# Routed rows finished one expert earlier, indirect transfers in written order, and four residual stores on another queue

## The chip, the cores and the metric

One core of one Trainium2 chip. The metric is the device time of one execution in microseconds; the number before is the median of three runs. The trace is one profiled execution of the same program.

## The reference, cut to what matters

One layer of an encoder trunk on 512 tokens (and 16 meta tokens) of width 1024. After the mixer and its layer norm comes a mixture of experts and a second layer norm, and the change is in that last part alone:

```python
grp_score = lax.top_k(grp, TOP_K)[0].sum(-1)      # 4 groups of 4 experts
sel = jnp.argmax(grp_score, axis=-1)              # one group for a token
topv, topi = lax.top_k(jnp.where(in_grp, scores, -1.0), TOP_K)   # two experts of it
for e in range(N_EXPERTS):                        # 16
    h = jax.nn.silu(t @ w_gate[e]) * (t @ w_up[e])
    out = out + comb[:, e:e + 1] * (h @ w_down[e])
h = layer_norm(DN_ALPHA * h + ffn, ln2_g[i], ln2_b[i])
```

Both experts of a token are of one group, so experts of different groups have no token in common.

## The kernel before, in words

The mixture works expert by expert, at most 96 tokens of each in the main path. `order` (L935) takes one expert of each group in turn (0, 4, 8, 12, 1, 5, ...), so four neighbours in it belong to four groups; below, "expert 12" means place 12 of `order`, and 15 is the last. For each place the kernel gathers the token rows from `h1_dram` into `XG` (L1505, an indirect DMA from GpSimd), transposes them (`xprep`, L1113) into `xT` (`x_out`, L1076: four parts on ScalarE, four on VectorE), multiplies by the gate and up weights (`gu`, L1101, and `gu_third` for tokens 65 to 96, in a branch on the count), applies silu (`act`, L1148), transposes the result (`htr`, L1274, copied to `hT` by ScalarE), multiplies by the down weights (`down`, L1299) and adds the weighted result to `o_dram` by two indirect DMAs that accumulate (`add_rows`, L1350). The weights stream from DRAM on SyncE's queue (`fetch`, L1239) into slots of 1 MB that are reused in turn.

`o_dram` first receives the residual rows: four tiles of 128 tokens, scaled on VectorE and stored from GpSimd (L1205 to L1208). `XG[0]` is then set to zero (L1253) and the rows of place 2 are gathered into it.

At the end the second layer norm is made by the class `Finish` (L1409). `out` already holds the bias of the norm, and each result is added to it by a scattering DMA. The four token tiles are loaded back from `o_dram` (L1530) after the scatters of place 12, normalised as a whole, and stored with the index `rest` (L1039), which sends the tokens of the last three experts out of bounds; the rows of places 13, 14 and 15 are gathered from `o_dram` (`rows_of`, L1555), normalised and stored by their own indices. From L1539 on VectorE and ScalarE execute in the order in which the code is written. In that order `xprep` of place 15 comes before the statistics of the tiles (L1565 to L1567), and the tiles' scaling on ScalarE (L1575) comes after `htr` of place 14. A scatter into `o_dram` waits until the tile loads have read it. The last expert is computed in split precision (`down_split`, L1323), whose two halves of output feed the last norm.

## Time and profile before

| | |
|---|---|
| median of three runs | 1038.21 us (1037.29 to 1038.98) |
| the profiled execution | 1038.58 us |
| its span in the trace | 1036.8 us |
| TensorE busy | 946.0 us, 91% of the span |
| mean granted TensorE clock | 0.969 |
| DMA over the whole span | 199.43 MB, 192 GB/s |

Times in the rows are microseconds from the span's start; busy and mean times of single instructions include their fixed part. The text in brackets at the end of a timeline row is the idle time of that engine before it and what ended it. L89 is the line of a helper that records instructions in written order, so those rows are told apart by their tiles: `gu` and `py` are the results of the gate or up and of the down products, `pt` transposes, `ys` the weighted rows, `raw` and `hb` the slots.

### The profile page before, as it was taken

What the parts mean: (1) busy time and instruction counts of PE and PEld (TensorE: products, weight loads), DVE (VectorE), ACT (ScalarE), POOL (GpSimd) and SP (SyncE); (2) the same over time, 40 slices, a digit from 0 to 9 for tenths busy, and PEclk for the clock granted to TensorE, in tenths of its full rate; (3) what the DMA queues carried; (4) which work ended last, traced back from release to release, by engine and by line L of the source; (5) the groups of instructions that cost most, each with busy time, mean ns of one, the idle gap of its engine ahead of it and who ended that gap; (6) DMA issues with size and microseconds to landing.
All of it is one profiled execution on the core that took longest, in us unless ns stands there. A gap on an engine that the chain in (4) does not pass through costs nothing. (4 is left out here: it accounts for less than half of the span.)

```text
span 1036.8 us, 19979 instructions
## 1 busy us (share of the span) xinstructions
PE 946.0 (91%) x8460; PEld 757.0 (73%) x8460; DVE 594.0 (57%) x1180; ACT 350.5 (34%) x503; POOL 167.5 (16%) x150
## 2 busy tenths in 40 slices
PE   4879999999999999999999897999779788999980
PEld 3878888999899898989898785877545344564550
DVE  6877671376869696978878778666520101001173
ACT  4344332532435252433425353224112121112252
POOL 4930000000000000000000226200212121212343
PEclk9999999999999999999999998999989899999996
DMA  7442446422323142333332423977899999999744
GB/s 220 138 162 100 131 131 178 122 82 82 134 90 128 56 151 74 123 102 123 102 122 72 153 91 133 379 290 304 293 367 372 373 373 374 371 372 373 251 123 78
DMA packets 98739, 199.43 MB, mean 192 GB/s; under 512 B 10272, under 2 KB 56968, under 8 KB 97616
## 3 DMA queue, kind: packets, MB, share of 16 engines
q1 hardware_dynamic: 83392, 163.78, 44.8%
q0 software_dynamic: 9392, 18.61, 7.2%
q10 hardware_dynamic: 5856, 15.61, 4.1%
q8 instruction: 76, 1.25, 0.5%
q14 instruction: 23, 0.19, 0.1%
HBM read 185.79 MB, written 19.79 MB: 198 GB/s over the span
## 5 line engine op out<-in xcount | busy, mean ns | idle before, releaser
L255 DVE TENSOR_TENSOR wl<-raw,wh 128x2048 fp32r<-128x2048 f32 (+1 forms) x49 | 111.7, 2283 | 53.2 <-ACT wh L252 53.0
L252 ACT CAST wh<-raw 128x2048 fp32r<-128x2048 f32 (+1 forms) x49 | 87.9, 1798 | 143.6 <-PE ss L800 64.1
L307 PE MATMUL mm<-hH,wh 128*128 128x264 f32 x624 | 128.7, 287 | 6.1 <-ACT ze L599 5.4
L89 PE MATMUL gu<-raw,xT 128*32 128x256 f32 (+1 forms) x2592 | 126.8, 344 | 7.8 <-issue 4.0
L307 PE MATMUL mm<-hH,wl 128*128 128x264 f32 x624 | 128.0, 286 | 0.0
L307 PE MATMUL mm<-hL,wh 128*128 128x264 f32 x624 | 127.3, 285 | 0.0
L89 PEld LDWEIGHTS gu<-raw,xT 128*32 128x32 f32 x2592 | 82.8, 110 | 48.8 <-issue 16.8
L1153 DVE TENSOR_TENSOR sg<-sg,gu 128x128 f32<-128x128 f32 x13 | 3.7, 288 | 182.5 <-ACT sg L1152 182.5
L307 PEld LDWEIGHTS mm<-hH,wh 128*128 128x128 f32 x624 | 99.1, 190 | 9.4 <-ACT ze L599 5.6
L809 POOL TENSOR_TENSOR acc<-acc,pre 128x512 f32<-128x512 f32 x12 | 19.1, 1614 | 530.5 <-ACT pre L808 530.5
L325 PE MATMUL mm<-hH,wh 128*128 128x512 f32 x256 | 102.5, 401 | 0.0
L325 PE MATMUL mm<-hL,wh 128*128 128x512 f32 x256 | 101.6, 397 | 0.0
L325 PE MATMUL mm<-hH,wl 128*128 128x512 f32 x256 | 101.5, 396 | 0.0
L307 PEld LDWEIGHTS mm<-hH,wl 128*128 128x128 f32 x624 | 98.0, 189 | 1.2 <-DVE wl L255 0.2
L307 PEld LDWEIGHTS mm<-hL,wh 128*128 128x128 f32 x624 | 97.4, 189 | 0.2
L89 PE MATMUL py<-raw,hT 128*32 128x512 f32 (+1 forms) x704 | 73.8, 558 | 5.2 <-issue 4.6
L800 PE MATMUL ss<-wh,yy 128*128 128x512 f32 x192 | 67.3, 410 | 0.0
L89 PEld LDWEIGHTS py<-raw,hT 128*32 128x32 f32 x704 | 23.5, 116 | 46.2 <-issue 39.2
L325 PEld LDWEIGHTS mm<-hH,wl 128*128 128x128 f32 x256 | 48.2, 188 | 10.5
L325 PEld LDWEIGHTS mm<-hH,wh 128*128 128x128 f32 x256 | 48.1, 188 | 10.3
L325 PEld LDWEIGHTS mm<-hL,wh 128*128 128x128 f32 x256 | 48.0, 188 | 10.3
L1256 POOL DMA_INDIRECT o_dram<-ys,ixq x26 | 40.5, 1557 | 74.3 <-ACT ys L1354 70.7
(391 smaller groups left out, 1584.1 us busy)
## 6 DMA issues: line engine op xcount, KB each, us to landing
raw<-in_w_exp_down_dram SPq DMA_DIRECT2D x30, 1024.0 KB
raw<-in_w_in_dram SPq DMA_DIRECT2D x28, 1024.0 KB
raw<-in_w_exp_up_dram SPq DMA_DIRECT2D x28, 1024.0 KB
raw<-in_w_exp_gate_dram SPq DMA_DIRECT2D x26, 1024.0 KB
M<-aD ACTq DMA_DIRECT2D x8, 1024.0 KB
raw<-in_w_in_dram SPq DMA_DIRECT2D x16, 512.0 KB
raw<-in_w_ssd_out_dram SPq DMA_DIRECT2D x8, 1024.0 KB
ze<-eD ACTq DMA_DIRECT2D x16, 256.0 KB
```

The source lines that it names most:

```text
L89: return lambda *a, **k: self.tc.keep_in_program_order(f(*a, **k))
L252: A.copy(wh[:, c], src[:, c])
L255: (E[i] if E else V).tensor_sub(wl[:, c], src[:, c], wh[:, c])
L307: T.matmul(ps[:, i, :HF], lhsT=w[:, k, cs], rhs=h[k][:, i * HF:(i + 1) * HF], start=(n == 0), stop=(n == 3 * KT - 1))
L325: T.matmul(ps, lhsT=w[:, k, cs], rhs=h[k][:, NM:], start=(n == 0), stop=(n == 3 * KT - 1))
L800: T.matmul(ps, lhsT=y[:, j, t * 128:(t + 1) * 128], rhs=w[:, j, hf * 512:(hf + 1) * 512], start=(n == 0), stop=(n == 5))
L809: G.tensor_add(a, a, f)
L1153: V.tensor_mul(sg[:, 256:384], sg[:, 256:384], p3[:, 128:])
L1256: return G.indirect_dma_start(out=dst, out_offset=off(ix), in_=src[:n], in_offset=None, **lim(dst), **kw)
```

## The change

Three things. The residual's four stores are issued by ScalarE instead of GpSimd. The tiles are loaded one expert earlier, after the scatters of place 11, and `rest` leaves out the tokens of the last four experts; the rows of place 12 are gathered and finished by themselves. And from the last gather of `h1_dram` on, the indirect DMAs of GpSimd are issued in the order of the code. With that the written order of VectorE and ScalarE changes: the statistics and scales of the tiles come first, ahead of `act` of place 14 and `xprep` of place 15, and the scaling of the four tiles comes ahead of `add_rows` of place 13.

```diff
@@ -258,12 +258,23 @@
         return bass.IndirectOffsetOnAxis(ap=ix, axis=0)
 
 
+
+    queue = []
+
+    def queued(f):
+        if not queue:
+            return f()
+        with tc.issue_after(queue[-1]):
+            r = f()
+        queue.append(r.ins)
+        return r
+
     def lim(v):
         return dict(bounds_check=v.shape[0] - 1, oob_is_err=False)
 
     def gather(dst, src, ix):
         n = ix.shape[0]
-        return G.indirect_dma_start(out=dst[:n], out_offset=None, in_=src, in_offset=off(ix), **lim(src))
+        return queued(lambda: G.indirect_dma_start(out=dst[:n], out_offset=None, in_=src, in_offset=off(ix), **lim(src)))
 
 
     with ExitStack() as p1:
@@ -1036,7 +1047,7 @@
 
             with tc.high_priority(offset=-3000):
                 rf, r1 = tokf[:, t:t + 1], small("rf")
-                for e_ in order[-3:]:
+                for e_ in order[-4:]:
                     o_ = rest[:, t:t + 1] if e_ == order[-1] else r1
                     V.scalar_tensor_tensor(o_, ohs[:, t, e_:e_ + 1], float(FAR), rf, op0=OP.mult, op1=OP.add)
                     rf = o_
@@ -1205,7 +1216,7 @@
             for t in range(NT):
                 V_.tensor_mul(vt[t], vt[t], g1B)
                 V_.tensor_add(vt[t], vt[t], b1B)
-                G.dma_start(o_dram[t * 128:(t + 1) * 128, :], vt[t])
+                A.dma_start(o_dram[t * 128:(t + 1) * 128, :], vt[t])
 
 
     rawz = ctx.enter_context(tc.tile_pool(name="rawz", bufs=RZ, reuse_waits="tile"))
@@ -1253,7 +1264,7 @@
     G.memset(XG[0], 0.0)
     def scatter(dst, src, ix, **kw):
         n = ix.shape[0]
-        return G.indirect_dma_start(out=dst, out_offset=off(ix), in_=src[:n], in_offset=None, **lim(dst), **kw)
+        return queued(lambda: G.indirect_dma_start(out=dst, out_offset=off(ix), in_=src[:n], in_offset=None, **lim(dst), **kw))
 
 
     gu3 = psG.tile([128, 256], F32, name="gu3", bufs=1)
@@ -1411,7 +1422,7 @@
 
 
         def __init__(self, rows, junk):
-            self.rows, self.junk, self.n = rows, junk, len(rows)
+            self.rows, self.junk, self.n = rows, junk, len(rows) + 1
 
             self.mv = mo.tile([128, self.n, 2], F32, name="mvf", bufs=1)
             self.rs = mo.tile([128, 4, self.n], F32, name="rsf", bufs=1)
@@ -1513,10 +1524,12 @@
         if i == 1:
             with tc.issue_after(last_[V]):
                 overflow()
+        if i == last - 2:
+            break
         add_rows(down(i - 1, fetch(wd[order[i - 1]], 256)), i - 1)
 
 
-    i, e = last - 1, order[last - 1]
+    w2, e = fetch(wd[order[last - 3]], 256), order[last - 1]
     wg2, wu2, w3 = fetch(wg[e], 512), fetch(wu[e], 512), fetch(wd[order[last - 2]], 256)
     wg_, wp_ = fetch(wg[order[last]], 512), fetch(wd[e], 256)
     wu_, wd_ = fetch(wu[order[last]], 512), fetch(wd[order[last]], 256)
@@ -1525,18 +1538,41 @@
     Q.dma_start(gb2[0], bcast_row(ln2_g, D))
     fv = [slot((128, 2, D)) for _ in range(4)]
     fv = [v[:, k, :] for v in fv for k in range(2)]
-
     for t in range(NT):
         last_['SP'] = Q.dma_start(fv[t], o_dram[t * 128:(t + 1) * 128, :]).ins
-    rows3 = fv[NT:NT + 3]
-    for v in rows3:
+    rows4 = fv[NT:]
+    for v in rows4:
         G.memset(v, 0.0)
-    gather(XG[(i + 1) % 2], h1_dram[:, :], ix_of(i + 1))
+    queue.append(gather(XG[last % 2], h1_dram[:, :], ix_of(last)).ins)
+
+
+    i = last - 1
+    V, A, G = (InOrder(tc, e_) for e_ in (V, A, G))
+
+    def rows_of(k, n):
+
+        ins = gather(rows4[k], o_dram[:, :], ix_of(last - 3 + k)).ins
+        if n:
+            apart(ins, n)
+        gets.append(ins)
+
+    def add_to(p, k):
+        for sc in add_rows(p, k):
+            for g_ in gets:
+                tc.declare_no_dep(sc, g_, reason="experts of different groups have no token in common")
+
+    gets = []
+    fin = Finish(fv[:NT] + rows4[:3], None)
+    add_to(down(i - 2, w2), i - 2)
+    rows_of(3, 1)
+    rows_of(0, 0)
+    for t in range(NT):
+        fin.stats(t)
+    fin.scales(slice(0, NT))
     pg = gu(wg2)
     count(i)
     htr(hs.pop(i - 1))
     pu = gu(wu2)
-    V, A, G = (InOrder(tc, e_) for e_ in (V, A, G))
     hs[i] = act(pg, pu, p3=gu_third(i, (wg2, wu2)))
     xprep(XG[(i + 1) % 2])
     us = [[slot((128, 2, D), F32R) for _ in range(2)] for _ in range(2)]
@@ -1546,71 +1582,63 @@
     spare = [spare[:, 2 * k:2 * k + 2] for k in range(2)]
     after = nu[0]
     on = spare[1]
+    fin.rows.append(fl(on))
+    fin.junk = fl(spare[0])
+    for t in range(NT):
+        fin.scaled(t)
+        fin.gain(t)
+    fin.store(0, rest[:, 0:1])
+    add_to(down(i - 1, w3), i - 1)
+    for t in range(1, NT):
+        fin.store(t, rest[:, t:t + 1])
     V.memset(fl(on)[CAP:], 0.0)
-    for w, (wh, wl) in zip(wd_, us):
-        A.copy(wh, w)
-        V.tensor_sub(wl, w, wh)
-    add_rows(down(i - 1, w3), i - 1)
-
-    def rows_of(k, ins, n):
-
-        ins.append(gather(rows3[k], o_dram[:, :], ix_of(last - 2 + k)).ins)
-        return ins[-1]
-
-    gets = []
-    apart(rows_of(2, gets, 2), 2)
-    rows_of(0, gets, 0)
-    fin = Finish(fv[:NT] + rows3[:2] + [fl(on)], fl(spare[0]))
-    tiles = slice(0, NT)
-    for t in range(NT):
-        fin.stats(t)
-    fin.scales(tiles)
+
+    def part(k):
+        A.copy(us[k][0], wd_[k])
+        V.tensor_sub(us[k][1], wd_[k], us[k][0])
+
+    part(0)
+    fin.stats(NT)
+    fin.scales(slice(NT, NT + 1))
     pg = gu(wg_)
     count(last)
     htr(hs.pop(i))
     sg = silu(pg)
-    for sc in add_rows(down(i, wp_), i):
-        for g_ in gets:
-            tc.declare_no_dep(sc, g_, reason="experts of different groups have no token in common")
-    for t in range(NT - 1):
-        fin.scaled(t)
-        fin.gain(t)
-    for t in range(2):
-        fin.store(t, rest[:, t:t + 1])
-    rows_of(1, gets, 0)
+    part(1)
+    add_to(down(i, wp_), i)
+    rows_of(1, 1)
+    fin.scaled(NT)
+    fin.gain(NT)
+    fin.store(NT, ix_of(last - 3))
+    rows_of(2, 0)
     act(None, gu(wu_), p3=gu_third(last, (wg_, wu_)), sg=sg)
     htr_split(sg, hhl)
     A.activation(epsq, epsc, AF.Sqrt)
     py = down_split(us, hhl)
-    fin.scaled(NT - 1)
-    fin.gain(NT - 1)
-    for t in range(2, NT):
-        fin.store(t, rest[:, t:t + 1])
-    fin.sums(NT)
-    fin.stats(NT + 1)
-    two, end = slice(NT, NT + 2), slice(NT + 2, NT + 3)
-    w_, og, st = col_of(wsl, last)[:CAP], rows3[2], bn_tile()
+    fin.sums(NT + 1)
+    fin.scales(slice(NT + 1, NT + 2))
+    fin.scaled(NT + 1)
+    fin.stats(NT + 2)
+    w_, og, st = col_of(wsl, last)[:CAP], rows4[3], bn_tile()
+    for hf in range(2):
+        V.scalar_tensor_tensor(on[:CAP, hf, :], py[hf], w_, og[:CAP, hf * 512:hf * 512 + 512], op0=OP.mult, op1=OP.add)
+        V.bn_stats(st[:, hf, :], on[:, hf, :])
+        if not hf:
+            fin.gain(NT + 1)
+            fin.store(NT + 1, ix_of(last - 2))
+    V.bn_aggr(fin.mv[:, NT + 3, :], st)
+    two = slice(NT + 2, NT + 4)
     fin.root(two)
-    V.scalar_tensor_tensor(on[:CAP, 0, :], py[0], w_, og[:CAP, 0:512], op0=OP.mult, op1=OP.add)
-    V.bn_stats(st[:, 0, :], on[:, 0, :])
     fin.steps(two)
-    V.scalar_tensor_tensor(on[:CAP, 1, :], py[1], w_, og[:CAP, 512:], op0=OP.mult, op1=OP.add)
-    V.bn_stats(st[:, 1, :], on[:, 1, :])
-    fin.scaled(NT)
-    V.bn_aggr(fin.mv[:, NT + 2, :], st)
-    fin.root(end)
-    fin.gain(NT)
-    fin.store(NT, ix_of(last - 2))
-    fin.steps(end)
-    fin.scaled(NT + 1)
-    fin.gain(NT + 1)
-    fin.store(NT + 1, ix_of(last - 1))
-
-    A.activation(og, fl(on), AF.Identity, bias=fin.rs[:, 3, NT + 2:NT + 3], scale=fin.rs[:, 0, NT + 2:NT + 3])
-    fin.rows[NT + 2] = og
-    fin.gain(NT + 2)
-    fin.store(NT + 2, ix_of(last))
+
+    A.activation(og, fl(on), AF.Identity, bias=fin.rs[:, 3, NT + 3:NT + 4], scale=fin.rs[:, 0, NT + 3:NT + 4])
+    fin.rows[NT + 3] = og
+    fin.scaled(NT + 2)
+    for n in (3, 2):
+        fin.gain(NT + n)
+        fin.store(NT + n, ix_of(last - 3 + n))
     V, A, G, Q, T = plain
+    queue.clear()
     with tc.issue_after(last_['SP']):
         last_['SP'] = Q.dma_start(gb2[1], bcast_row(ln2_b, D)).ins
 
```

## Rows read from the trace of the kernel before

**Rows 1.** The page: its span.

```profile
span 1036.8 us, 19979 instructions
```

**Rows 2.** Timeline of TensorE (PE), places 1 to 3: start, us, what, idle before.

```profile
739.52 0.55 PE L89 MATMUL pt<-ident,sg 128*128 128x128 f32 x3
...
746.11 1.58 PE L89 MATMUL gu<-raw,xT 128*32 128x128 f32 x49 [0.28 <-issue]
...
756.94 1.53 PE L89 MATMUL pt<-ident,xg 96*128 96x96 f32 x8 [9.25 <-DMA xg<-h_dram,idx]
...
764.51 1.90 PE L89 MATMUL gu<-raw,xT 128*32 128x256 f32 x32
...
775.63 1.20 PE L89 MATMUL pt<-ident,xg 96*128 96x96 f32 x8
...
781.95 3.64 PE L89 MATMUL gu<-raw,xT 128*32 128x256 f32 x64
```

**Rows 3.** Timeline of GpSimd (POOL) in the same stretch.

```profile
746.69 0.97 POOL L1253 MEMSET xg<- 128x1024 f32 x1
...
747.94 1.01 POOL L266 DMA_INDIRECT xg<-h_dram,idx  x1 [0.28 <-POOL xg L1253]
```

**Rows 4.** Stretches: length, busy of PE, PEld, DVE, ACT, POOL, clock, DMA share, GB/s.

```profile
735.00:966.00 231.00, 203.27 (x3279) 117.66 (x3283) 36.57 (x116) 43.62 (x113) 55.84 (x45) 0.94 1.03 373
...
966.00:979.00 13.00, 11.14 (x163) 6.08 (x155) 1.85 (x6) 3.49 (x9) 5.45 (x5) 1.00 0.61 227
...
808.50:815.00 6.50, 6.46 (x32) 2.45 (x36) 1.85 (x6) 1.67 (x5) 1.01 (x1) 0.51 1.03 408
```

**Rows 5.** Timeline of SyncE's queue (SP), the last loads.

```profile
960.70 1.98 SPq L1525 DMA_DIRECT2D raw<-in_ln_g_dram  x1
...
981.28 2.41 SPq L1530 DMA_DIRECT2D raw<-o_dram  x4
```

**Rows 6.** Timeline of GpSimd (POOL), scatters of places 11 and 13.

```profile
958.58 1.55 POOL L1256 DMA_INDIRECT o_dram<-ys,ixq  x1 [0.30 <-issue]
...
991.50 1.56 POOL L89 DMA_INDIRECT o_dram<-ys,ixq  x1 [12.29 <-DMA raw<-o_dram]
```

**Rows 7.** Timeline of VectorE (DVE), place 14 and the tiles.

```profile
983.04 1.24 DVE L89 TENSOR_SCALAR xT<-pt,gb 128x96 f32<-128x96 f32 x4 [0.63 <-PE pt L89]
...
994.47 1.23 DVE L89 BATCH_NORM_STATS2 st<-raw 128x6 f32<-128x512 f32 x2
...
995.73 0.21 DVE L89 BATCH_NORM_AGGREGATE mvf<-st 128x2 f32<-128x12 f32 x1
```

**Rows 8.** Timeline of ScalarE (ACT), places 13 and 14.

```profile
983.89 3.71 ACT L89 CAST raw<-raw 128x2048 fp32r<-128x2048 f32 x2
...
992.32 0.48 ACT L89 COPY hT<-pt 128x384 f32<-128x384 f32 x1 [3.48 <-PE pt L89]
...
996.56 1.05 ACT L89 ACTIVATE ys<-py,wq 128x512 f32<-128x512 f32 x2 [3.48 <-PE py L89]
...
998.36 3.51 ACT L89 ACTIVATE raw<-raw,rsf 128x1024 f32<-128x1024 f32 x3 [0.75 <-DVE rsf L89]
```

**Rows 9.** Timeline of TensorE (PE): down products, and the split one.

```profile
810.00 6.06 PE L89 MATMUL py<-raw,hT 128*32 128x512 f32 x32
...
992.85 3.64 PE L89 MATMUL py<-raw,hT 128*32 128x512 f32 x32 [0.62 <-ACT hT L89]
...
1007.32 5.80 PE L89 MATMUL pye<-raw 128*96 128x512 f32 x24 [1.60 <-ACT raw L89]
```

**Rows 10.** The last chain: ACT, DVE, DVE, then POOL.

```profile
1009.83 1.04 ACT L89 ACTIVATE raw<-hb 128x1024 f32<-128x1024 f32 x1
...
1012.53 0.73 DVE L89 SCALAR_TENSOR_TENSOR raw<-pye,wsl,raw 96x512 f32<-96x512 f32 x1
...
1019.91 1.23 DVE L89 TENSOR_TENSOR raw<-raw 128x1024 f32<-128x1024 f32 x1 [0.22 <-ACTq L1623]
...
1022.75 1.43 POOL L89 DMA_INDIRECT out_dram<-raw,idx  x1 [0.30 <-issue]
```

## The prediction

> **What bounds the kernel now.** I read the page first [rows 1]: the span is 1036.8 us, the profiled time 1038.58 us, so 1.78 us lie outside it; the profile is 0.37 us above the median of 1038.21 us. TensorE is busy for 91% of the span, so the next view was its timeline. Through the experts it runs almost without a gap, with one exception: after the products of place 1 end at 747.69 it stands for 9.25 us until the rows `xg` of place 2 have come [rows 2]. GpSimd's timeline shows why: the memset of `XG[0]` starts at 746.69, right behind the last residual store, and the gather only at 747.94 [rows 3].
>
> The stretches show a second resource at its limit. From 735 to 966 us the DMA engines are busy 1.03 of the time at 373 GB/s [rows 4]. Weights are fetched into slots well ahead, so in this profile TensorE does not wait for them; but the stream has an end of its own. Its last load, the gain of the norm, is issued at 960.70 [rows 5], and the transfers thin out between 966 and 979 us, 13 us at 227 GB/s, 2.95 MB [rows 4]. I read 979 as the time when the stream has landed.
>
> At the end TensorE leads: the copy of `hT` of place 14 ends at 992.80 [rows 8], its down product starts at 992.85, and the split product runs from 1007.32 to 1013.12 [rows 9]. After that a chain of VectorE and ScalarE ends at 1021.14 and GpSimd's last store is issued by 1024.18; the span ends 12.62 us later [rows 10, 1].
>
> **The change, part by part.**
>
> *Stores on ScalarE's queue.* ScalarE idles where they go, so issuing them costs nothing: its next work, the `hT` copy of place 0, has to wait for the same VectorE results. If that cover were missing, four issues would stand there, which cost SyncE 2.41 us for four loads [rows 5]. GpSimd loses four issues, and with them the waits ahead of the memset. The memset then needs only the transposes of `htr` of place 0, over at 740.07 [rows 2]: memset 740.1 to 741.1, gather 0.28 us later at 741.35 [rows 3]. From its start to TensorE's start took 9.00 us before (747.94 to 756.94). With the same 9.00 us the rows land at 750.35, 6.6 us earlier; at best they land before 747.7 and all 9.25 us go. Then the clock: from `xprep` to the next `gu` took 7.57 us after the gap and 6.32 us one place later [rows 2], so 1.25 us more. The gain at place 2 is 7.8 to 10.5 us; I take 9, for the data no longer stand behind 2 MB of stores in their own queue.
>
> The trace has these stores and the weights in flight together, at a busy share of 1.03 [rows 4]. The Trainium skill (DMA: Bandwidth & Descriptors, "Issuing engines are not separate DMA queues") says that DMAs of all issuing engines share the same 16 DMA engines, so that another issuer saves only sequencer time. By that rule the 9.00 us stay and only the earlier issue counts. That is the lower end above.
>
> *The tiles one expert earlier.* Scatter 11 is issued by 960.13 [rows 6], or some 9 us sooner, so its landing no longer decides. The four loads follow the gain of the norm on SyncE's queue, behind the stream that ends at 979. Price: 4 x 524,288 bytes at 408 GB/s, which a stretch of mere loads reached [rows 4], are 5.14 us: **the last tile lands at 984.1**. Lower end: if they fill the thin 13 us completely, (2.95 + 2.10 MB) at 373 GB/s after 966 give 979.5. Upper end: before, the scatter that waits for these loads started 10.22 us after their issue [rows 5, 6], which behind 979 gives 989.2. I take 984.1, as the loads queue behind a running stream and not into idle engines.
>
> Now VectorE's order counts. Statistics and scales stand ahead of `act` of place 14 and of `x_out` of place 15, which before ran at 983.04 [rows 7]. A tile's statistics take 1.47 us from first start to last end; the last tile is through at about 986.0. From there to ScalarE's first scaling went 2.42 us (995.94 to 998.36) [rows 7, 8]: 988.4. `x_out` comes after the scales, so TensorE, which with its 9 us would want it at about 979, stands until about 989.
>
> ScalarE's order is the longer chain. Four scalings at 1.17 us (three took 3.51): 993.1. `ys` of place 13, 1.05 us: 994.1. Half of the two casts, 1.86 us: 996.0. The `hT` copy of place 14, 0.48 us: 996.5 instead of 992.80 [rows 8]. **The down product of place 14 starts 3.7 us later than before, and the 9 us are gone.** What VectorE does meanwhile (gains, memset, one subtraction) is shorter than this chain and than TensorE's next products.
>
> *Clock.* TensorE now has idle stretches of some 8 and 3 us there. After the branch gap ahead of 808.5, the clock was 0.51, the 1.2 GHz level, from 808.5 to 815, and a down product of 32 matmuls took 6.06 us instead of 3.64 [rows 4, 9]. Between 0 and that I take the row: +2.4 us.
>
> *The tail.* B is the start of the split product (1007.32 before). The gathers of places 13 and 14 and GpSimd's longer row of stores end ahead of their users, as the tiles' stores are issued during the products. Before, the sums began at B + 2.5, after one scaling that is now gone, so now at about B + 1.5; two passes of 1.04 us [rows 10] with their small steps make some 2.6 us. Then VectorE in written order: scales of place 13 (bounded by the 2.42 us above; 2.2), statistics of place 14 (1.47): the first half of the last rows starts at B + 7.7, not B + 5.21 [rows 10]. From there to the end of the gain were 8.61 us; one block of six small steps (0.9) goes, a gain (1.2) moves off the root's shadow into the row; I take 8.2. Then a store starts at B + 16.2, a second one behind it ends at B + 19.5 instead of B + 16.86. With 12.0 us to the span's end (12.62 before, with more stores in flight) that is B + 31.5 instead of B + 29.5: +2.0 us, between 0 (if the sums and scales hide) and 3.
>
> `rest` with one more step per tile, a fourth memset, and a fourth gathered set of rows cost 0: they lie beside products. If the memset were late, only a gather would wait.
>
> **Sum:** 1038.58 + 3.7 + 2.4 + 2.0 = 1046.7 us on the profile's scale, 1046.3 on the median's. Its own range is 1039.5 (tiles at 979.5, clock kept) to 1051.4 (tiles at 989.2).
>
> **The rivals.**
>
> *The tiles are not late.* If the loads overtake the last weights, or the stream follows TensorE and ends 9 us sooner while VectorE fits its 8 us in ahead of place 14, the 9 us survive. For it: the slots come free earlier. Against: a share of 1.03 leaves the stream no room, and the loads stand last in the queue. It decides at about 976: from there down the kernel is faster, and below 969 nothing of the stall is left: 1038.2 - 9 + 2 = 1031, with part of the chain left up to 1036. Chance 0.20.
>
> *They land at the lower end, and the clock holds:* 1038.2 + 3.7 - 4.6 + 2.0 = 1039.3, no change that can be told. For it: the thin 13 us have room for all four tiles. Against: the transfers end on single engines, and a tile needs all. Chance 0.12.
>
> *The moved stores don't free the gather* (the memset or the rows wait for something else). Then TensorE comes to place 15 as before, at 983, waits for VectorE only some 6 us and keeps its clock: 1046.3 - 2.4 = 1043.9. Chance 0.10.
>
> **How the numbers follow.** The forecast has 0.58. A measurement of this kernel can tell some 0.2%, 2.1 us, from no change. Faster: the first rival, 0.20. Same: the second and the low edge of the forecast, 0.14. Slower: the rest, 0.66. The range must reach into the first rival, as 0.20 plus the top would be too much to leave out: 1034 to 1051.
>
> **What would show it.** Right: TensorE's 9.25 us gap gone or small; SyncE's tile loads issued about 963; the last tile's statistics at about 984; a gap of TensorE ahead of the second half of `gu` of place 15 until about 989, with the clock at 0.5; `hT` of place 14 copied at about 996; the split product from about 1013; the last store of GpSimd near 1033. Wrong: statistics of the tiles ending before 977, or a copy of `hT` of place 14 before 990; then the gain of place 2 reaches the end.

## The result, and the profile after

The changed kernel takes **1047.51 us** (median of four runs, 1046.83 to 1049.04) where the kernel before takes 1038.6 us beside it (1037.29 to 1040.06): ratio 1.0088, 95% interval 1.0073 to 1.0103. It is slower, as forecast, 1.2 us above the predicted 1046.3 and inside the range. The profiled execution took 1046.83 us, of which 1044.7 us are span, 7.9 us more than before [rows 1]. The page of the changed kernel:

```profile
span 1044.7 us, 20003 instructions
```

The two profiled executions do not start even. TensorE begins place 1 (the first `gu` of the expert loop) at 733.92 us after and at 735.92 us before; the change reaches nothing ahead of that. One row of the kernel before that the earlier groups do not hold, TensorE's timeline:

```profile
735.92 3.66 PE L89 MATMUL gu<-raw,xT 128*32 128x256 f32 x64 [1.07 <-ACT xT L1082]
```

So times within the experts are told below also as S+t, where S is that start (735.92 before, 733.92 after). TensorE's timeline of the changed kernel, from place 1 to the split product:

```profile
733.92 3.66 PE L89 MATMUL gu<-raw,xT 128*32 128x256 f32 x64 [1.07 <-ACT xT L1093]
...
748.09 1.49 PE L89 MATMUL pt<-ident,xg 96*128 96x96 f32 x8 [2.13 <-DMA xg<-h_dram,idx]
...
755.76 1.90 PE L89 MATMUL gu<-raw,xT 128*32 128x256 f32 x32
...
968.98 3.66 PE L89 MATMUL gu<-raw,xT 128*32 128x256 f32 x64 [0.34 <-DMA raw<-o_dram]
...
987.30 3.55 PE L89 MATMUL gu<-raw,xT 128*32 128x256 f32 x32 [2.21 <-DVE xT L89]
...
994.24 5.21 PE L89 MATMUL py<-raw,hT 128*32 128x512 f32 x32 [2.91 <-ACT hT L89]
...
1009.43 5.79 PE L89 MATMUL pye<-raw 128*96 128x512 f32 x24 [1.60 <-ACT raw L89]
```

At place 2 the gap is 2.13 us instead of 9.25 [rows 2], and the transposes of `xg` stand at S+14.17 instead of S+21.02. At the end stand two new waits that before did not have: 2.21 us for VectorE's `xT` inside `gu` of place 15, and 2.91 us for ScalarE's `hT` ahead of the down product of place 14. The split product starts at 1009.43, which is S+275.51 instead of S+271.40.

GpSimd's and ScalarE's timelines at place 1, then the last of VectorE's four residual tiles and the load of gate weights that SyncE issued last ahead of them:

```profile
738.13 0.95 POOL L1264 MEMSET xg<- 128x1024 f32 x1 [4.00 <-PE pt L89]
...
739.35 1.71 POOL L277 DMA_INDIRECT xg<-h_dram,idx  x1 [0.27 <-POOL xg L1264]
...
736.73 11.81 ACTq L1219 DMA_DIRECT2D o_dram<-v  x4
...
748.64 0.48 ACT L1291 COPY hT<-pt 128x384 f32<-128x384 f32 x1 [14.76 <-DMA raw<-in_w_exp_gate_dram]
...
742.65 1.22 DVE L89 TENSOR_TENSOR v<-v,b1B 128x1024 f32<-128x1024 f32 x1
...
731.79 0.37 SPq L228 DMA_DIRECT2D raw<-in_w_exp_gate_dram  x1
```

GpSimd sets `XG[0]` to zero as soon as TensorE's transposes are through and issues the gather at 739.35, 8.6 us sooner than before [rows 3], 6.6 by S. ScalarE stands among the four store issues for 11.81 us, and its copy of `hT` comes at 748.64. The row of 11.81 us is mostly waiting: in the trace each issue takes 0.33 us, the first three (736.73, 739.12, 741.51) start within 0.05 us of VectorE's tiles, and the fourth starts at 748.21 although its tile is ready at 743.87. What ended that last wait was the landing, at 748.14, of the gate weights that SyncE had issued at 731.79: by the trace the fourth store waits for the semaphore that this load counts up.

The tile loads on SyncE, and then the chain of VectorE and ScalarE that follows from them:

```profile
961.82 6.65 SPq L1542 DMA_DIRECT2D raw<-o_dram  x4
```

```profile
978.23 1.28 DVE L89 BATCH_NORM_STATS2 st<-raw 128x6 f32<-128x512 f32 x2 [13.54 <-SPq L1651]
...
983.73 0.21 DVE L89 BATCH_NORM_AGGREGATE mvf<-st 128x2 f32<-128x12 f32 x1
...
986.34 0.62 DVE L89 TENSOR_TENSOR sg<-sg,gu 128x256 f32<-128x256 f32 x2
...
986.87 1.23 DVE L89 TENSOR_SCALAR xT<-pt,gb 128x96 f32<-128x96 f32 x4
...
986.45 4.64 ACT L89 ACTIVATE raw<-raw,rsf 128x1024 f32<-128x1024 f32 x4 [7.38 <-DVE rsf L89]
...
993.71 0.47 ACT L89 COPY hT<-pt 128x384 f32<-128x384 f32 x1
```

The statistics start at 978.23, when the first tile has landed. (SyncE's L1651, which the profile names there, waits for the same landing; by these waits the last weights landed at 975.70, the gain of the norm at 976.96 and the first tile at 978.23, in the order of SyncE's queue.) They run without a gap for 5.7 us, and `act` of place 14 and the rows of place 15 come only behind the scales, at 986.34 and 986.87. ScalarE's scalings, `ys` of place 13 and half a cast follow one another to the copy of `hT` at 993.71. Of the stretches below, the first is the thin end of the stream with the tiles in it, the second what follows it, the last two the wait and the down product of place 14 (length, busy time of PE, PEld, DVE, ACT and POOL, granted clock, DMA share, GB/s):

```profile
966.00:979.00 13.00, 12.48 (x175) 6.59 (x171) 0.77 (x2) 3.42 (x9) 0.00 (x0) 0.97 0.82 326
...
979.00:985.00 6.00, 6.00 (x92) 2.61 (x81) 5.69 (x16) 0.08 (x1) 1.95 (x2) 1.00 0.18 44
...
985.00:994.20 9.20, 4.11 (x39) 1.69 (x35) 8.66 (x20) 7.75 (x9) 7.71 (x4) 0.81 0.26 52
...
994.20:999.60 5.40, 5.21 (x32) 1.15 (x32) 4.72 (x10) 2.13 (x3) 4.62 (x3) 0.70 0.79 130
```

With the tiles in it the thin end of the stream runs at 326 GB/s instead of 227 [rows 4], and behind 979 little is left. In the down product of place 14 the clock is 0.70, between its two levels.

The tail, GpSimd first, then ScalarE and VectorE:

```profile
982.74 1.55 POOL L89 DMA_INDIRECT o_dram<-ys,ixq  x1 [20.61 <-DMA raw<-o_dram]
...
1010.15 1.00 POOL L89 DMA_INDIRECT hb<-o_dram,idx  x1 [0.30 <-issue]
...
1013.94 1.01 POOL L89 DMA_INDIRECT raw<-o_dram,idx  x1 [1.02 <-DMA o_dram<-ys,ixq]
...
1014.30 1.06 ACT L89 ACTIVATE raw<-hb 128x1024 f32<-128x1024 f32 x1 [3.41 <-DMA hb<-o_dram,idx]
...
1016.99 0.15 DVE L89 TENSOR_SCALAR rsf<-mvf 128x1 f32<-128x1 f32 x1 [7.29 <-ACT raw L89]
...
1020.57 0.74 DVE L89 SCALAR_TENSOR_TENSOR raw<-pye,wsl,raw 96x512 f32<-96x512 f32 x1
```

GpSimd stands until 982.74, as its scatters of place 12 wait for the tile loads, and is then busy almost without a pause until the gather of place 14's rows at 1013.94. The rows of place 13 are gathered at 1010.15, and ScalarE's sums wait 3.41 us for them. The first half of the last rows starts at 1020.57, 11.1 us after the split product, where before it was 5.2 us [rows 9, 10]. From the start of the split product to the span's end go 35.3 us instead of 29.5.

The 7.9 us are thus, from front to back: 2.0 us gained ahead of place 1, 4.1 us lost from there to the split product, 5.8 us lost behind it.

### The profile page after: what moved, and what is told of

The parts are those of the page before. It is cut to its first block, busy times and chain, and to the rows that moved or that the text cites. A ratio compares the mean times of both kernels' runs of the same rounds, so it can differ in the third digit from the quotient of the medians.

```text
span 1044.7 us, 20003 instructions
## 1 busy us (share of the span) xinstructions
PE 952.4 (91%) x8460; PEld 757.5 (73%) x8460; DVE 598.3 (57%) x1200; ACT 351.0 (34%) x503; POOL 174.4 (17%) x149
## 3 DMA queue, kind: packets, MB, share of 16 engines
q8 instruction: 76, 1.25, 0.5%
## 5 line engine op out<-in xcount | busy, mean ns | idle before, releaser
L89 PE MATMUL py<-raw,hT 128*32 128x512 f32 (+1 forms) x704 | 78.4, 586 | 8.3 <-issue 5.2
L1267 POOL DMA_INDIRECT o_dram<-ys,ixq x24 | 37.3, 1553 | 71.0 <-ACT ys L1365 67.3
```

Of the source, the lines that this page charges most:

```text
L89: return lambda *a, **k: self.tc.keep_in_program_order(f(*a, **k))
L1267: return queued(lambda: G.indirect_dma_start(out=dst, out_offset=off(ix), in_=src[:n], in_offset=None, **lim(dst), **kw))
```

## The experiments

All times of a stage in this table come from the one profiled execution of each kernel, the ratio from its timed runs against the kernel before on the same chip. "hT" is the start of ScalarE's copy of place 14, "split" the start of the split product, "tail" from there to the span's end.

| kernel | S | hT | split | tail | median us | ratio, 95% interval |
|---|---|---|---|---|---|---|
| before | 735.92 | S+256.4 | S+271.4 | 29.5 | 1038.6 | |
| changed | 733.92 | S+259.8 | S+275.5 | 35.3 | 1047.5 | 1.0073 to 1.0103 |
| changed, again | 734.89 | S+258.6 | S+275.9 | 34.9 | 1049.3 | 1.0061 to 1.0129 |
| moved stores alone | 734.20 | S+249.3 | S+264.2 | 30.9 | 1034.2 | 0.9938 to 0.9981 |
| moved stores alone, again | 740.02 | S+252.2 | S+266.4 | 31.7 | 1035.6 | 0.9931 to 0.9976 |
| stores back | 737.20 | S+262.2 | S+278.9 | 35.1 | 1051.5 | 1.0079 to 1.0130 |
| rows of 13 first | 736.00 | S+259.5 | S+277.7 | 32.9 | 1048.6 | 1.0057 to 1.0105 |
| tiles behind | 733.74 | S+251.2 | S+277.4 | 38.6 | 1051.5 | 1.0082 to 1.0136 |
| VectorE back | 734.74 | S+260.7 | S+280.2 | 32.0 | 1049.1 | 1.0050 to 1.0115 |
| tiles by GpSimd | 736.93 | S+254.7 | S+269.3 | 36.8 | 1044.8 | 1.0027 to 1.0066 |
| rows of 13 second | 733.91 | S+258.9 | S+276.8 | 35.0 | 1050.0 | 1.0066 to 1.0135 |
| stores last | 735.24 | S+260.1 | S+275.8 | 32.1 | 1046.4 | 1.0042 to 1.0083 |
| all orders changed | 736.68 | S+249.0 | S+263.1 | 39.9 | 1040.1 | 0.9978 to 1.0035 |

### The two halves of the change apart

The kernel before with the moved stores and nothing else:

```diff
-                G.dma_start(o_dram[t * 128:(t + 1) * 128, :], vt[t])
+                A.dma_start(o_dram[t * 128:(t + 1) * 128, :], vt[t])
```

> Theory (the moved stores give TensorE time at place 2, and the new order at the end takes it away): the gap ahead of the transposes of place 2 falls from 9.25 us to about 2, TensorE is 5 to 7 us ahead from there, and since before's order at the end is led by TensorE, the lead reaches the end: 1031 to 1034 us. Rival (the weight stream has an end of its own, and a TensorE that is ahead only waits for weights): the lead melts until place 14, and the time stays at 1037 to 1039 us.

It takes 1034.17 us, 0.996 of the kernel before. TensorE's timeline, and the stretch in which the stream thins out:

```profile
748.06 1.17 PE L89 MATMUL pt<-ident,xg 96*128 96x96 f32 x8 [1.53 <-DMA xg<-h_dram,idx]
...
984.03 3.64 PE L89 MATMUL py<-raw,hT 128*32 128x512 f32 x32 [0.62 <-ACT hT L89]
...
998.42 7.10 PE L89 MATMUL pye<-raw 128*96 128x512 f32 x24 [1.60 <-ACT raw L89]
```

```profile
966.00:979.00 13.00, 12.82 (x187) 6.99 (x183) 4.75 (x8) 6.17 (x10) 3.79 (x3) 1.00 0.68 230
```

The gap at place 2 is 1.53 us, and in this profile the lead is there to the end: the down product of place 14 starts at S+249.8 instead of S+256.9, the split product 7.2 us sooner. The rival's melting lead does not happen here, though the stream thins out in the same stretch as before (230 GB/s; 227 before [rows 4]): the stream does have its own end, but in the old order no wait of TensorE at the end names it. Once more, on another chip:

> The moved stores alone once more, beside the kernel with all orders changed: 1032 to 1036 us, 3 to 6 us below the kernel before. By the rival (the first result owed itself to one chip) it is within 2 us of the kernel before.

1035.57 us, 0.9953 of the kernel before. In this second profile the split product is only 5.0 us sooner by S, so how much of the lead arrives differs between executions; the times agree: **the moved stores are worth some 4 to 5 us, and alone they make a kernel that is faster than both.** The other half alone is the changed kernel with the stores on GpSimd again:

> Theory (the tiles' loads behind the weight stream set when place 14 and 15 go on, so TensorE's lead is worth nothing in this order): the 9 us gap of place 2 is back, the tiles' statistics still end at 983 to 986 us, the split product starts within 1.5 us of the changed kernel's 1009.4, and the time is 1046 to 1049 us. Rival (part of the lead still reaches the end): the split product starts 4 to 6 us later and the time is 1051 to 1054 us.

1051.52 us. The rival was right that part of the lead reaches the end: by S the split product starts 3.0 to 3.4 us later than in the two profiles of the changed kernel. By medians the lead is worth 2.2 to 4.0 us (1049.3 and 1047.5 us for the changed kernel, each on another chip), and the intervals of the ratios overlap, so the stages carry this reading. Timelines of TensorE, SyncE, GpSimd and VectorE:

```profile
758.52 1.52 PE L89 MATMUL pt<-ident,xg 96*128 96x96 f32 x8 [9.17 <-DMA xg<-h_dram,idx]
...
971.65 2.44 SPq L1542 DMA_DIRECT2D raw<-o_dram  x4
...
962.07 1.55 POOL L1267 DMA_INDIRECT o_dram<-ys,ixq  x1 [0.30 <-issue]
...
988.12 1.23 DVE L89 BATCH_NORM_STATS2 st<-raw 128x6 f32<-128x512 f32 x2
```

The tile loads are issued at S+234.5, against S+227.9 in the changed kernel, and the last tile's statistics start at S+250.9 instead of S+248.5. The scatters of place 11, which they read after, are issued up to 963.62 here, and the loads are issued 8 us after that; in the changed kernel these scatters are out by 953.80 and the loads start at 961.82, again 8 us later. So the loads wait for TensorE's progress as well as for the stream. By medians the rewritten end costs 12.7 us with the stores on GpSimd (1051.5 against 1038.8 on the same chip) and 13.3 us with them on ScalarE (1047.5 against 1034.2).

### What the changed kernel does twice

> The changed kernel once more, beside the next three on one chip, to tell what differs from one execution to the next: 1046 to 1049 us; the copy of hT of place 14 at 993 to 996 us and 33 to 36 us from the start of the split product to the end of the span.

1049.3 us, `hT` and tail as expected. Five runs lie between 1046.8 and 1053.7, so single results below are read to some 2 us, and by stages.

### Which of the two chains holds place 14

Only VectorE's order undone:

```diff
-    for t in range(NT):
-        fin.stats(t)
-    fin.scales(slice(0, NT))
     pg = gu(wg2)
...
     xprep(XG[(i + 1) % 2])
+    for t in range(NT):
+        fin.stats(t)
+    fin.scales(slice(0, NT))
```

> Only VectorE's order undone: act of place 14 and the rows of place 15 ahead of the tiles' statistics and scales; ScalarE's scalings stay ahead of ys of place 13 and of the hT copy of place 14. Theory (ScalarE's row of scalings, ys and half cast is the longer of the two chains): TensorE's gap in gu of place 15 goes, the gap ahead of the down product of place 14 grows by as much, hT is copied within 1 us of where the changed kernel has it, and the time is within 2 us of the changed kernel's. Rival (VectorE's block is what costs): hT copied 3 us or more sooner, and the time 3 to 5 us below the changed kernel's.

```profile
995.99 6.54 PE L89 MATMUL py<-raw,hT 128*32 128x512 f32 x32 [8.12 <-ACT hT L89]
```

The theory held in the main: the wait in `gu` of place 15 is gone, the one ahead of the down product is 8.12 us instead of 2.91 (4.54 in the changed kernel's second profile), `hT` comes no sooner (0.9 to 2.1 us later by S, where within 1 us was expected), and the time is the changed kernel's, 1049.1 against 1049.3 us on the same chip. **Place 14 waits for ScalarE's row.** The down product then takes 6.54 us, and the split product is 4.3 to 4.7 us later, but the tail is 2.9 to 3.2 us shorter, probably as GpSimd has caught up meanwhile; no run isolates that. Now ScalarE's scalings behind the copy of `hT` as well, on the changed kernel:

```diff
-    for t in range(NT):
-        fin.scaled(t)
-        fin.gain(t)
-    fin.store(0, rest[:, 0:1])
     add_to(down(i - 1, w3), i - 1)
-    for t in range(1, NT):
-        fin.store(t, rest[:, t:t + 1])
...
     part(0)
+    for t in range(NT):
+        fin.stats(t)
+    fin.scales(slice(0, NT))
...
     sg = silu(pg)
+    for t in range(NT):
+        fin.scaled(t)
+        fin.gain(t)
+    fin.store(0, rest[:, 0:1])
+    for t in range(1, NT):
+        fin.store(t, rest[:, t:t + 1])
     part(1)
```

> Statistics and scales of the tiles behind the rows of place 15 on VectorE, their scalings behind the hT copy of place 14 on ScalarE; all else as in the changed kernel. Theory (place 14's down product waits for ScalarE's scalings, and the tail for GpSimd's queue): TensorE's gap ahead of gu of place 15 is gone, hT of place 14 is copied at 987 to 990 us instead of 993.7, the split product starts 3 to 5 us sooner (1005 to 1006.5); GpSimd's stores of the tiles come later, so the rows of place 13 are not gathered sooner, and the time falls by under 2 us: 1045.5 to 1047.5. Rival (the end simply follows the split product): 1042.5 to 1044.5 us. Second rival (the weights of place 15 are what TensorE would wait for): the split product starts within 1.5 us of 1009.4.

```profile
984.91 0.48 ACT L89 COPY hT<-pt 128x384 f32<-128x384 f32 x1 [1.69 <-PE pt L89]
...
1000.29 6.83 DVE L89 TENSOR_TENSOR raw<-raw 128x1024 f32<-128x1024 f32 x5
...
1008.64 0.90 PE L89 MATMUL pt<-ident,sg 128*128 128x128 f32 x3 [10.32 <-DVE sg L89]
```

`hT` comes at 984.91, S+251.2, 8.6 us sooner than in the changed kernel. Both orders are changed here, but VectorE's block moved alone had gained nothing, so ScalarE's row is what had to go. But the kernel takes 1051.52 us, which neither theory nor rivals gave. VectorE's block has only moved: the tiles' gains stand with one subtraction in a row to 1007.1, `act` of place 15 behind them, and TensorE waits 10.32 us for it. A written order needs a place for these 13 us of VectorE (8.1 of statistics and scales, 4.6 of gains) on every path.

### When the tiles land

The four tile loads from GpSimd's queue instead of SyncE's:

```diff
-    Q.dma_start(gb2[0], bcast_row(ln2_g, D))
+    last_['SP'] = Q.dma_start(gb2[0], bcast_row(ln2_g, D)).ins
...
-        last_['SP'] = Q.dma_start(fv[t], o_dram[t * 128:(t + 1) * 128, :]).ins
+        G.dma_start(fv[t], o_dram[t * 128:(t + 1) * 128, :])
```

> The four loads of the tiles issued by GpSimd instead of SyncE, so that they do not stand behind the weights in SyncE's queue. Theory (the queue's order makes the tiles late): the first statistics start at 972 us or sooner instead of 978.2, the last end by 978, hT of place 14 is copied 5 us or more sooner, and the time is 1040 to 1043 us. Rival (the engines that carry the transfers are full until about 975 us, share 1.01 to 0.86, whatever the queue, and loads moved ahead only push weights back): the statistics still end at 982 to 986 us, and the time is 1046 to 1049 us.

```profile
972.35 1.29 DVE L89 BATCH_NORM_STATS2 st<-raw 128x6 f32<-128x512 f32 x2 [4.85 <-DMA raw<-o_dram]
...
980.17 1.29 DVE L89 BATCH_NORM_STATS2 st<-raw 128x6 f32<-128x512 f32 x2 [1.13 <-DMA raw<-o_dram]
...
991.65 0.48 ACT L89 COPY hT<-pt 128x384 f32<-128x384 f32 x1
```

GpSimd issues the first of the loads at 965.42, S+228.5, no sooner than SyncE does (S+227.9). Yet the first statistics start at S+235.4 instead of S+244.3 (S+243.1 in the changed kernel's second profile), the last tile's at S+243.2 instead of S+248.5 (S+247.3), and `hT` is copied 3.9 to 5.1 us sooner by S. The split product gains 6 us, 1.6 of them as the down product keeps its 3.64 us; the tail is 1.5 to 1.9 us longer. The time is 1044.8 us, 2.7 us below the changed kernel's first median and 4.5 below its second on the same chip. That lies between the two forecasts, 1.8 us above the theory's 1040 to 1043 and 1.2 below the rival's 1046 to 1049; the stages bear out the theory's cause at somewhat less than its size. So the place behind the weights in SyncE's queue is what makes the tiles late, by 4 to 5 us for the last of them. The rival's other half happened too: the last weights land at S+245.7 instead of S+241.8, and no wait of TensorE names them. The Trainium skill (DMA: Bandwidth & Descriptors, "Issuing engines are not separate DMA queues") has it that another issuing engine saves sequencer time only; here it let four transfers pass a queue of weights, with the DMA engines full.

### The tail

In the changed kernel the gather of place 13's rows moved ahead of the scatters of place 14:

```diff
+    rows_of(1, 0)
     add_to(down(i, wp_), i)
-    rows_of(1, 1)
```

> Theory (the tail is longer because the rows of place 13 are gathered late: in GpSimd's written order they stand behind the two scatters of place 14): with the gather ahead of these it is issued at about 1006.5 us instead of 1010.2, the sums start some 2 to 3.4 us sooner, and the time is 1044 to 1045.5 us. Rival (the gather of place 14, which then goes 1 us later, or VectorE's written order holds the end): no change, 1047 to 1048 us.

```profile
1011.15 0.28 ACT L89 ACTIVATE sg<-gu 128x128 f32<-128x128 f32 x1 [7.55 <-remote]
...
1015.10 1.04 ACT L89 ACTIVATE raw<-hb 128x1024 f32<-128x1024 f32 x1
```

The sums, in the second line, no longer wait, and the tail is 32.9 us. But the split product started 2.2 us later by S, and the time did not fall: 1048.6 us. About as much is a wait of TensorE, 2.21 us instead of 0.34, for the silu of place 15's third block (the first line), which starts 1.9 us behind the products that it reads and for which the profile names no engine; why stays open. Then ahead of three of the tile stores as well:

```diff
+    rows_of(1, 0)
     for t in range(1, NT):
         fin.store(t, rest[:, t:t + 1])
...
     add_to(down(i, wp_), i)
-    rows_of(1, 1)
```

> The gather of place 13's rows ahead of three of the four tile stores in GpSimd's queue. Theory (it came late, and ScalarE's sums waited 3.4 us for it): it is issued by 1003 us, the sums start within 2 us of the split product's start, and the stretch from that start to the span's end is 32 to 33.5 us instead of 35.3; where the split product starts as in the changed kernel, the time is 2 to 3 us below the changed kernel's of the same chip. Rival (a gather ahead of the other queue entries costs elsewhere what it gains, as the split product of the earlier try started 4.3 us later): the time is within 1 us of the changed kernel's or above.

```profile
1001.62 1.27 POOL L89 DMA_INDIRECT hb<-o_dram,idx  x1 [3.12 <-DMA o_dram<-ys,ixq]
...
1019.58 1.29 DVE L89 BATCH_NORM_STATS2 st<-raw 128x6 f32<-128x512 f32 x2 [2.57 <-DMA raw<-o_dram,idx]
```

The gather waits 3.12 us for the scatters that it reads after, all behind it in the queue go later, and now VectorE's statistics of place 14's rows wait 2.57 us for theirs. The tail stays at 35.0 us, the time at 1050.0: the rival. It is the queue and not one gather. Hence the tile stores behind what the tail waits for:

```diff
-    fin.store(0, rest[:, 0:1])
     add_to(down(i - 1, w3), i - 1)
-    for t in range(1, NT):
-        fin.store(t, rest[:, t:t + 1])
...
     rows_of(1, 1)
+    for t in range(2):
+        fin.store(t, rest[:, t:t + 1])
     fin.scaled(NT)
     fin.gain(NT)
+    rows_of(2, 0)
+    for t in range(2, NT):
+        fin.store(t, rest[:, t:t + 1])
     fin.store(NT, ix_of(last - 3))
-    rows_of(2, 0)
```

> The changed kernel with the four tile stores behind the scatters of place 14 and the gather of place 13 in GpSimd's queue, two of them ahead of the gather of place 14 and two behind it; the other engines as in the changed kernel. Theory (the tail is longer since GpSimd's queue brings the rows of both places 13 and 14 late): neither the sums of place 13 nor the statistics of place 14 wait for a gather, the stretch from the start of the split product to the span's end is 31.5 to 33 us instead of 35, and the time is 1044 to 1046.5 us. Rival (VectorE's and ScalarE's written order sets the tail, whatever GpSimd brings): the stretch stays at 34.5 us or more, and the time at 1047 to 1050 us.

```profile
1011.08 5.80 PE L89 MATMUL pye<-raw 128*96 128x512 f32 x24 [1.60 <-ACT raw L89]
...
1012.45 1.04 ACT L89 ACTIVATE raw<-hb 128x1024 f32<-128x1024 f32 x1
...
1017.25 1.29 DVE L89 BATCH_NORM_STATS2 st<-raw 128x6 f32<-128x512 f32 x2
```

Neither line has a wait any more, the tail is 32.1 us, and the time 1046.4 us, 2.9 us below the changed kernel's second median and 1.1 below its first. **The late rows were worth 3 us of tail.**

### All of it together

Tile loads by GpSimd, both orders changed, the gather of place 13 ahead of the scatters of place 14, the tile stores behind these, and the rows of place 12 finished behind the split product:

```diff
     add_to(down(i - 1, w3), i - 1)
     V.memset(fl(on)[CAP:], 0.0)
...
+    for t in range(NT):
+        fin.stats(t)
+    fin.scales(slice(0, NT))
     part(0)
...
     sg = silu(pg)
+    for t in range(NT):
+        fin.scaled(t)
+        fin.gain(t)
     part(1)
+    rows_of(1, 0)
     add_to(down(i, wp_), i)
+    for t in range(2):
+        fin.store(t, rest[:, t:t + 1])
+    rows_of(2, 0)
+    for t in range(2, NT):
+        fin.store(t, rest[:, t:t + 1])
     act(None, gu(wu_), p3=gu_third(last, (wg_, wu_)), sg=sg)
     htr_split(sg, hhl)
+    fin.stats(NT)
+    fin.scales(slice(NT, NT + 1))
+    A.activation(epsq, epsc, AF.Sqrt)
+    py = down_split(us, hhl)
     fin.scaled(NT)
     fin.gain(NT)
     fin.store(NT, ix_of(last - 3))
...
```

> The statistics of the tiles stay one expert earlier, but all that the runs so far blame is taken off the path: the tiles' loads go out from GpSimd, act of place 14 and the rows of place 15 come ahead of the statistics on VectorE, the four scalings come behind the hT copy of place 14 on ScalarE, the statistics of place 12's rows behind the split of place 15's, and GpSimd gathers place 13's rows ahead of the scatters of place 14 and stores the tiles behind them. Theory (these three orders are the whole loss against the old end with the moved stores): hT of place 14 is copied at 984 to 987 us, the split product starts at 997 to 1001, the span ends 31 to 34 us later, and the time is 1031 to 1037 us, as with the moved stores alone. Rival (the rows of one more expert are too much work for VectorE and GpSimd in the last 50 us in any order): the split product starts 4 us or more later, or its tail stays above 35 us, and the time is 1040 us or more.

```profile
999.79 7.35 PE L89 MATMUL pye<-raw 128*96 128x512 f32 x24 [1.60 <-ACT raw L89]
...
998.34 1.01 POOL L89 DMA_INDIRECT hb<-o_dram,idx  x1 [3.16 <-DMA o_dram<-ys,ixq]
...
1008.06 1.01 POOL L89 DMA_INDIRECT raw<-o_dram,idx  x1 [0.30 <-issue]
...
1013.36 1.29 DVE L89 BATCH_NORM_STATS2 st<-raw 128x6 f32<-128x512 f32 x2 [3.49 <-DMA raw<-o_dram,idx]
```

Half of the theory held: `hT` at S+249.0 and the split product at S+263.1 are where the moved stores alone have them, or ahead of it (S+249.3 and S+264.2, in their second profile S+252.2 and S+266.4). So the queue of the tile loads and the written orders together are the whole loss up to the split product. The other half fell: the tail is 39.9 us, the time 1040.1 us, 4.5 us above the moved stores alone on the same chip. GpSimd's gather of place 13 waits 3.16 us, the gather of place 14 goes out at 1008.06 behind two tile stores, and VectorE waits 3.49 us for its rows. The scaling of place 12's rows, now behind the split product, stands ahead of the sums as well. Why one more set of rows costs GpSimd this much even so, and whether another order of its entries would do, stays open: that was not tried.

### What the gather of place 2 waits for

The kernel before with `o_dram` filled at the start of the program, so that no stores are in flight at place 2; its result lacks the residual:

```diff
         packA = hd.tile([128, 128], F32, name="packA")
+        for t in range(NT):
+            G.dma_start(o_dram[t * 128:(t + 1) * 128, :], xt[t])
...
-                G.dma_start(o_dram[t * 128:(t + 1) * 128, :], vt[t])
```

> The kernel before without the residual's stores at place 1: its buffer is filled at the start of the program with the input's rows instead (so the residual is left out of the result), and nothing but weights and rows is in flight at place 2; the first phase starts later for it, so only place 2 is read. Theory (the weights alone keep the transfer engines full, so the rows of place 2 take their 9 us with or without the stores): from the start of the gather to TensorE's transposes 8 to 9 us, as in the changed kernel (8.74). Rival (the rows stand behind 2 MB of stores, and without these they come at once): 5 us or less, and TensorE does not wait for them.

```profile
742.99 1.71 POOL L266 DMA_INDIRECT xg<-h_dram,idx  x1 [0.27 <-POOL xg L1254]
...
750.29 1.17 PE L89 MATMUL pt<-ident,xg 96*128 96x96 f32 x8 [0.30 <-DMA xg<-h_dram,idx]
```

7.30 us in this one execution, against 8.4 to 8.9 us in the kernels with the stores on ScalarE and 9.00 before. Between the two numbers, near the theory: the stores in flight cost the rows 1 to 2 us, and the other 7.3 us are there without them. How much of these is the weights' doing, no run shows.

## Why the prediction was right, and where it was not

The direction was right by the mechanism forecast: tiles that land behind the weight stream, and behind them the written order. The terms were not all of the size given, and the total came so near because their errors cancel. On the profile's scale:

| term | predicted | measured, by S |
|---|---|---|
| `hT` of place 14 | +3.7 | +3.4 |
| lower clock, to the split product | +2.4 | +0.7 |
| tail | +2.0 | +5.8 |
| ahead of place 1 | 0 | -2.0 |
| sum | +8.1 | +7.9 |

*Moved stores.* The gather was to start at 741.35, S+5.43, and started at S+5.43. "I take 9, for the data no longer stand behind 2 MB of stores in their own queue" failed: the gather took 8.74 us, so 6.85 us were won at place 2, and the 6.6 us of the lower end, which left the 9.00 us as they were, were right; the stores' part is 1 to 2 us. The 1.25 us of clock on top did not come either: from the transposes to the next `gu` went 7.67 us, as before (7.57) [rows 2]. By place 14 (`gu` at 968.98; 973.92 before) the lead was only 2.9 us by S. In the other profiles with moved stores it was 3.2 to 8.4 us there; what takes the difference on the way, with the DMA engines full, was not settled. The rule that the prediction cites from the Trainium skill (DMA: Bandwidth & Descriptors, "Issuing engines are not separate DMA queues"), that another issuer does not speed up the data, agrees with this place: 8.74 us against 9.00.

*"Issuing them costs nothing."* The issues themselves were as cheap as forecast, 4 of 0.33 us, and VectorE's results cover them up to 743.87, as I said. What the prediction did not have is the 4.3 us that the fourth one then waited for the landing of a weight load: the copy of `hT` of place 0 came at S+14.7, where the kernel before has it at S+10.0. At the end that cost next to nothing, for TensorE's wait for `xg` covered it: its transposes start 0.55 us ahead of the copy, its down product 0.39 us behind the copy's end.

*Tiles behind the weights, and the written order.* Last statistics were to end at 986.0, the first scaling to start at 988.4, `hT` to be copied by 996.5: S+250.1, S+252.5 and S+260.6. They did so at 983.94, 986.45 and 994.18: S+250.0, S+252.5 and S+260.3. The experiments show each step: the queue (tiles by GpSimd), ScalarE as the longer chain (VectorE back), and the whole loss up to the split product (all orders changed, together with the queue).

*"Scatter 11 ... its landing no longer decides."* True only with TensorE's lead. The rival that the moved stores don't free the gather was priced by this step at 2.4 us below the forecast; the kernel that does just that is 2.2 to 4.0 us above the changed one.

*Clock.* The waits were 2.21 and 2.91 us, not some 8 and 3, and the clock in the down product of place 14 was 0.70: 5.21 us instead of 3.64 [rows 9], +1.6 us instead of +2.4. Another 0.9 us came back in the third block of place 15, which in the profile before had waits of its own.

*Tail.* "The gathers of places 13 and 14 and GpSimd's longer row of stores end ahead of their users" is the step that failed. GpSimd starts its row only at 982.74, when the tile loads have landed, and needs until 1015 for it. With the tile stores out of the way the tail was 32.1 us, 2.6 more than before, near the +2.0 of the estimate: 3.2 us are the queue.

*Ahead of place 1.* 2 us that no step held; it is not the change's. Without it the sum would have been off by 1.8 us, not 0.2, and the tail's 3.8 us too many were nearly made up by these 2.0 and the 1.7 us that the clock cost less: the near hit is in good part luck.

## What to carry to other kernels

A lead that one edit gives an engine is kept only if nothing later comes at a time of its own: before adding work in written order ahead of the path, list what that work waits for (here loads behind a full queue) and put it where the path has slack on every engine at once, not on the one that was looked at. Count the in-order queue of the engine that issues the indirect transfers like a compute engine, with a start time and a length. Read a row of several DMA issues one by one: most of its length may be waits between them. When a change is made of two edits, time them apart: here one of them was worth 4 to 5 us and the other cost 13.

## What the runs showed of the hardware

- Four store issues took 0.33 us each on ScalarE, but the fourth started 3.3 to 4.3 us after its data were ready in the eleven profiles with the stores there, held until an earlier load of weights from another queue, whose semaphore it shares, had landed: a DMA in a compute engine's row can stop that engine for a transfer that is not its own.
- The same four loads brought their first tile 7.7 to 8.9 us sooner from GpSimd than from SyncE's queue behind the weights, at the same busy share of the DMA engines (1.02 and 1.03 between S+228.0 and S+235.4); the last weights landed 3.9 us later.
- Two waits of TensorE, 2.21 and 2.91 us with some 4 us of work between, were followed by a down product of 5.21 us at a granted clock of 0.70; one wait of 8.12 us by 6.54 us. In the kernel with the tiles loaded by GpSimd one wait of 3.73 us left it at 3.64.
- The start of place 1, which no edit here reaches, lies between 733.7 and 740.0 us in 13 profiled executions, and at 734.20 and 740.02 in two of one kernel. Differences of a few microseconds are safer by stages than by spans.
